# Seven products instead of eight blocks in the remaining chunks of a down-projection

## The chip, the cores and the metric

The kernel runs on one core of one Trainium2 chip. The metric is the device time of one execution in microseconds; lower is better. The core has a matrix engine (TensorE, "PE" in the profile, with its weight loads as "PEld"), a vector engine (VectorE, "DVE"), a scalar engine (ScalarE, "ACT"), GpSimd ("POOL") and a queue processor (SyncE, "SP"). SP, ACT and POOL issue the transfers (DMAs) that move data between the chip's memory (HBM) and the core's.

## The reference

Two layers of an encoder work on x of 256 positions by 2048 channels, all in float32. Layer 0 has pooling and attention, layer 1 a matrix memory (mLSTM) scanned in both directions. Each is followed by the same gated MLP, and this case is about its last product:

```python
def conv_ffn(x, w_up, conv_w, conv_b, w_down):
    u = x @ w_up                                   # 2048 -> 2 * 5632
    up = jnp.pad(u, ((0, 0), (1, 1), (0, 0)))
    u = c[0] * up[:, :-2] + c[1] * up[:, 1:-1] + c[2] * up[:, 2:] + conv_b
    gate, val = jnp.split(u, 2, axis=-1)
    return (jax.nn.silu(gate) * val) @ w_down      # 5632 -> 2048
...
x = x + conv_ffn(rms_norm(x, norm_ffn[layer]), w_up[layer], ...)
```

The down-projection multiplies a 256 x 5632 matrix by a 5632 x 2048 one.

## The kernel before

**Numbers.** Every float32 operand is held as a high and a low part (`hl[:, 0]` and `hl[:, 1]`), and a product of two operands is three matmuls: high by high, high by low, low by high. Weights arrive as chunks `w` of 128 x 1024 floats (512 KB). `Stream.split` (lines 119 to 131) makes the parts: ACT copies the rounded high part (line 127), DVE subtracts it for the low part (line 128). There are six `w` buffers and four `hl` buffers; the program loads five chunks ahead of the one in use and splits two ahead.

**Order of the work.** TensorE's instructions stand in the order in which the Python program emits them. The other engines' orders are chosen by a scheduler at build time. Each engine works in its order. Small work that must be spread in time is fed through `Weave`, a clock that the emission moves on: a product counts 0.68, one k tile of an up-projection 0.645 (microseconds, as the program supposes them), and a task runs when its time on that clock has come.

**The MLP.** `ffn_layer` runs six chunks of the inner dimension, of 4, 8, 8, 8, 8 and 8 tiles of 128 (`FCH`). For each tile, `up` makes gate and value (64 matmuls), the convolution and the gate on ACT and DVE, and a tile of `g`. The down-projection of chunk c is put between the up-projections of chunk c+1, in slots that `_ffn_plan` lists; chunk 5 has its own tail (`down_two`, `down`) after them. A chunk is taken apart into pairs of tiles: two in chunk 0, four in the others. The 2048 output columns form two halves, h = 0 and h = 1, of two blocks of 512.

- **Directly** (`down`, tile `dn`): per pair and half, two tiles by two column blocks by two halves of the rows by three matmuls, that is 24 matmuls of 512 columns, and two chunks of weights. A chunk ends with four additions of 512 columns into x (line 437).
- **In seven products** (`unit`, tile `pp`; a Strassen-Winograd scheme on the 2 x 2 blocks of a pair): four products in a unit of kind A, three in kind B, 21 matmuls. The left-hand combinations (`combine`, line 1004 on) serve both halves. B needs one and a half chunks of plain weights per pair. A needs two chunks of weight combinations per pair, and these are made in two ways:
  - for h = 1 by `Sum` and `Chain`: SP loads one weight chunk into a `sum` tile, POOL issues a second DMA that adds another to it (lines 112 and 113; three `sum` buffers, prepared up to ten chunks ahead), and DVE then adds the sum to a third chunk (lines 123 and 124);
  - for h = 0 by `premix` (line 464 on): long before use, five DMAs per pair make both combinations in HBM (`m`): two copies from ACT's queue (512 KB each), then from POOL's an accumulating one of 512 KB and two of 256 KB (line 473). SP loads the finished chunks later as any other (`w<-m`). Each of the five waits, by `paced`, for the matmul emitted last before it.

The products of a unit stay in PSUM over all pairs of a chunk; `drain` then adds them to `acc` or x in seven steps per chunk and half (line 1070; the first use of an `acc` tile is a copy on ACT, line 1068), and `total` ends a half after chunk 4.

**Which half goes which way.** `_halves` (line 1227) gives h = 1 the seven products in chunks 0 to 4 of both layers. h = 0 gets them in chunks 2, 3 and 4 of layer 0 and 1 to 4 of layer 1 (`BOTH`) and is done directly in the rest. When both halves go this way, a unit takes two pairs, and the eight slots of a chunk are A, A, B, B for h = 1 and the same for h = 0; otherwise a unit takes one pair, and `down` is appended to some slots.

**When the premixing is done.** `premix(layer, gap, late)` gives pair i the start `min(i + 1, 8) * gap + max(i - 7, 0) * late` on the clock; its five DMAs stand 0.2, 1.2, 1.2 and 1.2 gaps apart. In layer 0 (gap 26, late 90) it starts after the first projection of the attention, in layer 1 (28, 28) with the mLSTM.

Of the kernel before, what the change touches and what calls it, by code (L numbers as in the profile page):

```python
# [31 lines left out]
FT = DFF // P  # L32
FCH = [4, 8, 8, 8, 8, 8]
CH = 8
BOTH = ((2, 3, 4), (1, 2, 3, 4))
NEG = -1.0e30
NGATE = 96 + 8
WARM = 5
# [171 lines left out]
def trunk(ctx: ExitStack, tc: tile.TileContext, gx, xT, xn, call, catt, cml, weights, mixes, out):  # L210
# [249 lines left out]
    def paced(ins):  # L460

        tc.add_manual_dep(ins.ins, last_mm[0].ins.name, now, reason="paced")

    def premix(layer, gap, late):

        def one(i, s0, s1, r, made):
            m = scratch.tile([P, 2, CH * P], F32, tag=f"m{layer}{i}", name=f"m{layer}_{i}")
            h = CH * P // 2
            steps = [(nc.scalar, m[:, 0], s0, {}, 0.2), (nc.scalar, m[:, 1], r, {}, 1.2),
                     (g, m[:, 0], s1, add, 1.2), (g, m[:, 1, :h], m[:, 0, :h], add, 1.2),  # L470
                     (g, m[:, 1, h:], m[:, 1, :h], add, 0.0)]
            for eng, to, src, kw, wait in steps:
                paced(eng.dma_start(to, src, **kw))
                if wait:
                    yield wait * gap
            for j in range(2):
                made[j].ap = m[:, j]

        for i, e in enumerate(mixes[layer]):
            wv.aside(one(i, *e), min(i + 1, 8) * gap + max(i - 7, 0) * late)  # L480


    def attention_layer(norm, nxt):
        with ExitStack() as es:
# [239 lines left out]
            catb.extend(actp.tile([P, 8, 2, S], F32R, tag=f"B{i}", name=f"cat{i}") for i in range(2))  # L724
            wv.add(k_block(ps))
            wv.tick(0.0)
            premix(0, 26.0, 90.0)
            with tc.manual_schedule(engines={mybir.EngineType.SP}):
                ps = mov_group(xx, "qproj0", after=squares)
            wv.add(q_block(ps, 0, 5.5))  # L730
# [231 lines left out]
    def ffn_layer(layer, norm, nxt):  # L962
        with ExitStack() as es:
# [188 lines left out]
            for kind, c, i, *j in _ffn_plan(layer):  # L1152
                if kind == "up":
                    if i == 0:
                        gts.append(actp.tile([P, 8, 2, S], F32R, tag=f"B{c % 2}", name=f"g{layer}_{c}"))
                    up(c, f, gts[c], i)
                    f += 1
                elif kind == "down":
                    down(c, i)
                elif kind == "two":  # L1160
                    down_two(c)
                elif kind == "mix":
                    combine(c, i)
                else:
                    unit(kind, c, i, *j)

    norms = [Norm(0), None]
    norms[1] = Norm(1)
    attention_layer(norms[0], norms[1])
    norms.append(Norm(2))  # L1170
    ffn_layer(0, norms[1], norms[2])
# [54 lines left out]

def _halves(layer, c):

    return () if c in (-1, len(FCH) - 1) else (0, 1) if c in BOTH[layer] else (1,)


def _ffn_plan(layer):

    seq = []
    for c, n in enumerate(FCH):
        pairs = FCH[c - 1] // 2 if c else 0  # L1240
        halves = _halves(layer, c - 1)

        if halves == (0, 1):
            slots = [[(kind, c - 1, h, js)] for h in (1, 0) for kind in "AB" for js in ((0, 1), (2, 3))]
        else:
            slots = [[(kind, c - 1, 1, (j,))] for kind in "AB" for j in range(pairs)]
            for b in range(2 if pairs else 0):
                slots[(b + 1) * pairs // 2 - 1].append(("down", c - 1, b))

        busy = {j: k for k, slot in enumerate(slots) for u in slot if u[0] == "A" for j in u[3]}  # L1250
        for i in range(n):
            seq.append(("up", c, i))
            seq += slots[i] if i < len(slots) else []
            if c < len(FCH) - 1:
                seq += [("mix", c, j) for j in range(n // 2) if i == max(2 * j + 1, busy.get(j, 0))]
    return seq + [("two", len(FCH) - 1, 0)] + [("down", len(FCH) - 1, b) for b in range(2, NB)]


def _down_chunks(layer, w):


    out, k0 = [], 0
    for c, n in enumerate(FCH):
        rows = w[k0 * P : (k0 + n) * P]
        blocks = [_mov(rows[:, b * 512 : b * 512 + 512]) for b in range(NB) if b // 2 not in _halves(layer, c)]
        if c == len(FCH) - 1:
            b0, b1 = blocks[:2]
            blocks[:2] = [b0[:-1], b1[:-1], b0[-1:], b1[-1:]]
        out += blocks
        k0 += n  # L1270
    n = sum(FCH[:-1]) // 2
    res = [np.concatenate(out)]

    def two(a, b):
        return np.concatenate([a, b], axis=2)

    for h in range(2):
        b = w[: 2 * n * P, 1024 * h : 1024 * h + 1024].reshape(n, 2, P, 2, 512)
        b11, b12, b21, b22 = (b[:, k, :, c] for k in range(2) for c in range(2))
        res += [two(b12, b12), two(b11, b22), two(b22, b21), two(b11, b21), two(b22[::2], b22[1::2])]  # L1280
    return res


def _ffn_weights(layer, up, parts):

    down = iter(parts[0])
    out, u, mixes = [], 0, []
    for kind, c, i, *j in _ffn_plan(layer):
        if kind == "up":
            out += up[u : u + 4]  # L1290
            u += 4
        elif kind in ("down", "two"):
            out += [next(down) for _ in range(FCH[c] // 2 * (2 if kind == "two" else 1))]
        elif kind != "mix":
            q0 = sum(FCH[:c]) // 2
            s0, s1, r, ba, bb = parts[1 + 5 * i : 6 + 5 * i]
            js = [q0 + e for e in j[0]]
            if kind == "B":
                last = bb[js[0] // 2]
                out += [ba[q] for q in js] + [last if len(js) == 2 else last[:, js[0] % 2 * 512 : js[0] % 2 * 512 + 512]]  # L1300
                continue
            for q in js:
                if i:
                    out += [Sum(s0[q], s1[q]), Chain(r[q])]
                else:
                    made = [Made(), Made()]
                    mixes.append((s0[q], s1[q], r[q], made))
                    out += made
    return out, mixes
# [103 lines left out]
```

## Time and profile before

| | us |
|---|---|
| median of 3 runs | 2169.69 (2166.5 to 2171.02) |
| profiled execution, its own time | 2166.59 |
| span of its profile | 2164.4 |
| PE busy in the span | 2158.2 (100%) |
| DVE busy | 1726.4 (80%) |
| ACT busy | 1407.6 (65%) |
| POOL busy | 129.5 (6%) |

The span runs from the first to the last instruction of the core; the execution's own time has 2.2 us around it. In the profile, `up` is a tile of an up-projection, `dn` a direct down-projection, `pp` one of the seven products, `m` a premixed chunk in HBM, `sum` a sum made on the way in. All matmuls have line 264, since one helper emits them. The MLP of layer 0 lies at about 257 to 976 us, that of layer 1 at about 1450 us to the end.

### The profile page before, as it was taken

How to read it: one execution, taken by the hardware profiler on the slowest of the kernel's cores; microseconds unless marked ns; L12 is line 12 of the kernel's file. 1: busy time of each engine (PE TensorE's matmuls, PEld its weight loads, DVE VectorE, ACT ScalarE, POOL GpSimd, SP SyncE). 2: the span in 40 equal slices, each digit the busy share in tenths (PEclk: the TensorE clock that was granted, in tenths of full speed). 3: DMA queues.
4: the chain of work that ended last, by engine and by line, in shares of the span. 5: the costliest groups of instructions: out<-in, count | busy, mean ns of one | idle time of the engine just before them, and what ended most of it. 6: DMA issues, size and time to landing. Idle time of an engine off the chain costs nothing.

```text
span 2164.4 us, 31559 instructions
## 1 busy us (share of the span) xinstructions
PE 2158.2 (100%) x11424; PEld 1847.8 (85%) x11424; DVE 1726.4 (80%) x2415; ACT 1407.6 (65%) x2204; POOL 129.5 (6%) x160
## 2 busy tenths in 40 slices
PE   9999999999999999999999999999999999999999
PEld 8888888888888888889888888888888888888887
DVE  7686688887988888986777677667889898988896
ACT  7665576766777767666454544457677777776763
POOL 0011010000000000000000010110000000000000
PEclk9999999999999999999999999999999999999999
DMA  9678989787988877767688888998979787887774
GB/s 324 216 205 256 288 249 261 227 276 241 296 268 290 280 257 231 252 192 225 204 248 250 250 245 240 274 281 255 270 208 286 256 283 244 267 262 252 230 252 162
DMA packets 158079, 543.73 MB, mean 251 GB/s; under 512 B 17658, under 2 KB 20258, under 8 KB 157922
## 3 DMA queue, kind: packets, MB, share of 16 engines
q1 hardware_dynamic: 129056, 459.74, 62.2%
q0 software_dynamic: 17440, 48.51, 13.8%
q10 hardware_dynamic: 11426, 33.47, 4.8%
q8 instruction: 89, 1.46, 0.3%
q14 instruction: 68, 0.56, 0.1%
HBM read 539.50 MB, written 60.86 MB: 277 GB/s over the span
## 4 chain that ended last, share of the span: by engine, by line
PE 97%; DMA 1%; DVE 1%; issue 0%; ACT 0%; DVEq 0%; POOLq 0%; ACTq 0%
PE up L264 44%; PE pp L264 13%; PE op L264 8%; PE dn L264 6%; PE mv L264 4%; PE mq L264 4%; PE mk L264 4%; PE mo L264 4%; PE qproj L264 3%; PE kproj L264 1%; PE vproj L264 1%; PE pool L264 1%; DVE hl L128 1%; DMA sum<-in_dn 1%; DMA w<-in_up 1%; PE qk L264 1%
## 5 line engine op out<-in xcount | busy, mean ns | idle before, releaser
L128 DVE TENSOR_TENSOR hl<-w,hl 128x1024 fp32r<-128x1024 f32 (+2 forms) x836 | 1001.7, 1211 | 227.2 <-ACT hl L127 224.7
L127 ACT CAST hl<-w 128x1024 fp32r<-128x1024 f32 (+2 forms) x835 | 856.3, 1043 | 453.1 <-PE up L264 149.2
L264 PE MATMUL up<-xx,hl 128*128 128x512 f32 (+1 forms) x5632 | 994.1, 337 | 0.1
L264 PEld LDWEIGHTS up<-xx,hl 128*128 128x128 f32 x5632 | 867.0, 188 | 131.0 <-DVE hl L128 0.5
L264 PE MATMUL pp<-hl,s 128*128 128x512 f32 x768 | 192.7, 392 | 0.0
L264 PEld LDWEIGHTS pp<-hl,s 128*128 128x128 f32 x768 | 141.6, 188 | 29.0
L264 PE MATMUL pp<-hl,g 128*128 128x512 f32 x576 | 148.0, 391 | 0.0
L427 ACT COPY tb_up<-up 128x512 f32<-128x512 f32 x88 | 51.7, 587 | 124.5 <-PE up L264 124.3
L264 PEld LDWEIGHTS pp<-hl,g 128*128 128x128 f32 x576 | 105.4, 188 | 20.8
L264 PE MATMUL dn<-hl,g 128*128 128x512 f32 x528 | 122.7, 390 | 0.0
L264 PEld LDWEIGHTS dn<-hl,g 128*128 128x128 f32 x528 | 98.7, 188 | 20.4
L993 ACT ACTIVATE y<-tb_up,conv 128x256 f32<-128x256 f32 x176 | 103.9, 590 | 0.0
L994 DVE TENSOR_TENSOR y<-y,z 128x510 f32<-128x510 f32 x88 | 60.7, 689 | 54.2 <-ACT y L993 54.2
L428 DVE TENSOR_TENSOR tb_up<-up,tb_up 128x512 f32<-128x512 f32 x88 | 60.8, 690 | 50.5 <-ACT tb_up L427 49.9
L264 PE MATMUL mk<-xx,hl 128*128 128x512 f32 (+1 forms) x512 | 92.2, 337 | 0.0
L264 PE MATMUL mq<-xx,hl 128*128 128x512 f32 (+1 forms) x512 | 92.1, 337 | 0.0
L264 PE MATMUL mv<-hl,xx 128*128 128x512 f32 (+2 forms) x480 | 91.7, 350 | 0.0
L264 PE MATMUL op<-hl,cat 128*128 128x512 f32 x384 | 91.7, 393 | 0.0
L991 ACT ACTIVATE z<-tb_up,conv 128x256 f32<-128x256 f32 x176 | 88.6, 503 | 4.4 <-DVE tb_up L986 3.1
L264 PE MATMUL mo<-hl,xx 128*128 128x512 f32 x384 | 90.5, 391 | 0.0
L264 PE MATMUL op<-hl,mcat 128*128 128x512 f32 x384 | 89.5, 392 | 0.0
L264 PEld LDWEIGHTS mq<-xx,hl 128*128 128x128 f32 x512 | 79.2, 188 | 11.6
(232 smaller groups left out, 2092.7 us busy)
## 6 DMA issues: line engine op xcount, KB each, us to landing
w<-in_up SPq DMA_DIRECT2D x352, 512.0 KB, 4.7
w<-in_dn SPq DMA_DIRECT2D x176, 512.0 KB, 4.5
w<-in_m_in SPq DMA_DIRECT2D x124, 512.0 KB, 5.8
m<-in_dn ACTq DMA_DIRECT2D x56, 512.0 KB, 6.2
w<-m SPq DMA_DIRECT2D x56, 512.0 KB, 4.8
w<-in_a_in SPq DMA_DIRECT2D x46, 512.0 KB, 5.6
sum<-in_dn SPq DMA_DIRECT2D x36, 512.0 KB, 5.2
sum<-in_dn POOLq DMA_DIRECT2D x36, 512.0 KB, 8.9
```

Source lines behind the costliest of these rows:

```text
L127: (self.nc.vector.tensor_copy if i + c == 0 else self.nc.scalar.copy)(hl[:, 0, c : c + n], w[:, c : c + n])
L128: low = self.nc.vector.tensor_sub(hl[:, 1, c : c + n], w[:, c : c + n], hl[:, 0, c : c + n].bitcast(F32))
L264: last_mm[0] = pe.matmul(out_, lhsT, rhs, start=start, stop=stop, skip_group_check=True)
L427: a.copy(tb, ps[:, :, 1, :])
L428: v.tensor_add(tb, ps[:, :, 0, :], tb)
L991: a.activation(z[:, 0, j, :], u[:, j, :], AF.Copy, scale=cw(tl, 0))
L993: a.activation(y[:, j, :], u[:, j, :], AF.Identity, scale=cw(tl, 1), bias=cw(tl, 3))
L994: v.tensor_add(y[:, :, 1:S], y[:, :, 1:S], z[:, 0, :, 0 : S - 1])
```

## The change

Both halves now take the seven products in chunks 0 to 4 of both layers. New for h = 0 are chunks 0 and 1 of layer 0 (six pairs) and chunk 0 of layer 1 (two pairs). `_ffn_plan` is made to cope with a chunk of two pairs, whose slots are then one A and one B per half. Layer 0 premixes 18 pairs instead of 12, and those from the ninth on follow each other by 42 instead of 90 on the clock. Layer 1 premixes 18 instead of 16, with the same gap.

```diff
-BOTH = ((2, 3, 4), (1, 2, 3, 4))
...
-            premix(0, 26.0, 90.0)
+            premix(0, 26.0, 42.0)
...
 def _halves(layer, c):
 
-    return () if c in (-1, len(FCH) - 1) else (0, 1) if c in BOTH[layer] else (1,)
+    return () if c in (-1, len(FCH) - 1) else (0, 1)
...
         if halves == (0, 1):
-            slots = [[(kind, c - 1, h, js)] for h in (1, 0) for kind in "AB" for js in ((0, 1), (2, 3))]
+            slots = [[(kind, c - 1, h, js)] for h in (1, 0) for kind in "AB"
+                     for js in ((0, 1), (2, 3))[: pairs // 2]]
```

## The prediction

> **What bounds the kernel now.** I read the busy times first, then the chain of work that ended last, then what TensorE waited for, its matmuls in order of time, and last the transfers.
>
> ```profile
> span 2164.4 us, 31559 instructions
> PE 2158.2 (100%) x11424; PEld 1847.8 (85%) x11424; DVE 1726.4 (80%) x2415; ACT 1407.6 (65%) x2204; POOL 129.5 (6%) x160
> ...
> PE 97%; DMA 1%; DVE 1%; issue 0%; ACT 0%; DVEq 0%; POOLq 0%; ACTq 0%
> PE up L264 44%; PE pp L264 13%; PE op L264 8%; PE dn L264 6%; PE mv L264 4%; PE mq L264 4%; PE mk L264 4%; PE mo L264 4%; PE qproj L264 3%; PE kproj L264 1%; PE vproj L264 1%; PE pool L264 1%; DVE hl L128 1%; DMA sum<-in_dn 1%; DMA w<-in_up 1%; PE qk L264 1%
> ```
> ```profile
> PEld up L264 <- DVE hl L128: 0.5, 1, 0.5
> ```
>
> TensorE is the bound and has no gaps: of the waits of its weight loads only one, 0.5 us, lies in the MLPs. So a matmul taken out is a matmul's time gained, as long as weights still arrive. The single wait tells where that is closest to failing. The chain leads it back to a `sum`, its accumulating half, and a slow weight load:
>
> ```profile
> 679.00 5.16 DMA sum<-in_dn
> 684.73 8.83 DMA sum<-in_dn
> 706.53 13.73 DMA w<-in_up
> 722.71 8.18 PE up L264 x46
> ```
>
> **What is saved on TensorE.** These are stretches of one kind from the chain, start and length:
>
> ```profile
> 267.83 46.67 PE up L264 x268
> 317.28 5.44 PE dn L264 x24
> 355.26 11.14 PE up L264 x64
> 368.45 55.72 PE up L264 x320
> 440.85 10.88 PE dn L264 x48
> 554.34 5.53 PE pp L264 x24
> 587.67 4.10 PE pp L264 x18
> ```
>
> The direct half costs 5.44 us for 24 matmuls, 227 ns each. A unit of two pairs costs 5.53 us in kind A and 4.10 us in kind B. A unit of one pair is what lies between two rows: A from 314.50 (267.83 + 46.67) to 317.28, 2.78 us; B from 366.40 (355.26 + 11.14) to 368.45, 2.05 us.
>
> - A chunk of two pairs before: 2 x 2.78 + 2 x 2.05 + 2 x 5.44 = 20.54 us. After: 2 x (5.53 + 4.10) = 19.26. Saved: 1.28, in each layer, so 2.56.
> - Chunk 1 of layer 0 before: 4 x (2.78 + 2.05) + 2 x 10.88 = 41.08 us. After: 4 x (5.53 + 4.10) = 38.52. Saved: 2.56.
>
> Together 5.1 us, from 24 matmuls fewer. In a sentence of its own: the Trainium skill, page TensorE: Matmul & The Clock Gate, section Back-to-back issue gap, gives about 131 ns as the sustained spacing at 512 columns. By it the saving would be an estimated 3.1 us (24 x 0.131); the trace differs (227 ns), and the sum goes by the trace.
>
> **What is added beside TensorE.**
>
> ```profile
> L128 DVE TENSOR_TENSOR hl<-w,hl 128x1024 fp32r<-128x1024 f32 (+2 forms) x836 | 1001.7, 1211 | 227.2 <-ACT hl L127 224.7
> L127 ACT CAST hl<-w 128x1024 fp32r<-128x1024 f32 (+2 forms) x835 | 856.3, 1043 | 453.1 <-PE up L264 149.2 <-PE op L264 64.2 <-PE mo L264 38.4
> L1070 DVE TENSOR_TENSOR acc<-acc,pp 128x512 f32<-128x512 f32 x52 | 34.4, 680 | 0.0
> ```
> ```profile
> core 0: us, PE busy (x) PEld busy (x) DVE busy (x) ACT busy (x) POOL busy (x), PEclk, DMA share, GB/s
> 313.00:398.00 85.00, 85.00 (x462) 73.15 (x461) 69.33 (x95) 60.64 (x100) 6.73 (x8) 1.00 0.89 259
> 540.00:668.00 128.00, 128.00 (x685) 109.70 (x685) 112.66 (x148) 94.11 (x144) 6.70 (x8) 1.00 0.86 282
> 668.00:798.00 130.00, 129.94 (x691) 110.95 (x690) 115.78 (x153) 95.02 (x146) 6.77 (x8) 1.00 0.87 279
> 798.00:926.00 128.00, 128.00 (x683) 109.69 (x682) 115.13 (x144) 90.98 (x136) 0.87 (x1) 1.00 0.73 238
> ```
>
> - Splits: eight pairs need 3.5 weight chunks instead of 2, twelve splits more. DVE gets 12 x 1.21 = 14.5 us and ACT 12 x 1.04 = 12.5. DVE's additions from PSUM grow by some nine (seven drains per chunk and half instead of four, with the copies for a first use done by ACT in either kernel): 6 us. On average this lies beside TensorE: the three later rows are stretches with both halves in seven products, DVE is at 88 to 90%, and TensorE waits 0.06 us in 386. The same load is what chunks 0 and 1 get. Cost 0. If that cover went, the splits of A slots would be late first.
> - PSUM: the products use the four `ps` banks, and the drains finish during the next up-projection as they do now. Cost 0.
> - SP: twelve more loads' worth of weights. They pass through the same six buffers, at the mean rate of the three later rows. Cost 0 taken alone.
> - Premixing: eight pairs more, each two copies on ACT's queue and three accumulating DMAs on POOL's, and in layer 0 more than twice as dense from the ninth pair on. ACT and POOL wait for a matmul before each; the scheduler put them where ACT would wait anyway, and 56 such copies stand in ACT's order now with no wait of TensorE from it. Their issue costs 0. What the transfers do to others is the open cost.
>
> **The open cost: who meets the denser premixing.**
>
> ```profile
> w<-in_dn SPq DMA_DIRECT2D x176, 512.0 KB, 4.5
> m<-in_dn ACTq DMA_DIRECT2D x56, 512.0 KB, 6.2
> sum<-in_dn SPq DMA_DIRECT2D x36, 512.0 KB, 5.2
> sum<-in_dn POOLq DMA_DIRECT2D x36, 512.0 KB, 8.9
> m<-in_dn POOLq DMA_DIRECT2D x28, 512.0 KB, 8.4
> ...
> q1 hardware_dynamic: 129056, 459.74, 62.2%
> q0 software_dynamic: 17440, 48.51, 13.8%
> ```
>
> POOL's queue (q0) takes 13.8 / 48.51 = 0.284% per MB, the loads' (q1) 62.2 / 459.74 = 0.135: an accumulated byte costs the transfer engines 2.1 times a loaded one.
>
> Three sums of an h = 1 unit are prepared a whole chunk early; the fourth waits for the first buffer to come free, and that is tight. DVE and then POOL around it, in chunk 3's first two slots:
>
> ```profile
> 677.76 1.22 DVE L128 TENSOR_TENSOR hl<-sum,hl 128x1024 fp32r<-128x1024 f32 x1
> ...
> 693.58 0.69 DVE L123 TENSOR_TENSOR w<-w,sum 128x512 f32<-128x512 f32 x1 [2.17 <-DMA sum<-in_dn]
> ...
> 700.94 1.22 DVE L128 TENSOR_TENSOR hl<-w,hl 128x1024 fp32r<-128x1024 f32 x1
> ```
> ```profile
> 701.24 2.22 PE L264 MATMUL pp<-hl,s 128*128 128x512 f32 x9
> ```
> ```profile
> 418.20 0.81 POOL L473 DMA_DIRECT2D m<-in_dn  x1 [27.05 <-PE up L264]
> ...
> 513.66 0.81 POOL L473 DMA_DIRECT2D m<-in_dn  x1 [27.54 <-PE up L264]
> ...
> 675.29 0.81 POOL L473 DMA_DIRECT2D m<-m  x1 [32.45 <-PE up L264]
> 684.73 0.87 POOL L113 DMA_DIRECT2D sum<-in_dn  x1 [8.62 <-DMA sum<-in_dn]
> ```
>
> The buffer is free at 679.0, DVE wants the sum at 691.4 (693.58 - 2.17): 12.4 us. SP's half and POOL's half take 5.2 and 8.9 at the median, 14.1 with nothing between them. Here an `m` of 256 KB left POOL at 675.29 just ahead, and the sum came 2.17 us late. TensorE did not feel that at once: the split that follows from it ended at 702.16 (700.94 + 1.22), and the matmuls that use it begin 1.38 us (a quarter of the 5.53) after 701.24, at 702.62. So the lead is 2.17 + 0.46 = 2.6 us; what a sum is late beyond that, TensorE waits.
>
> Now where the premix falls. The two POOL rows at 418.20 and 513.66 are the ninth and tenth pair, 95.5 us apart for a step of 90, so the clock runs 1.06 slow and a step of 42 is 44.6 us. The ninth pair starts 48 earlier (250 instead of 298), so its POOL copy is at 367; the next ones at 412, 456, 501, 546, 590, 635, 679, 724, 768, each with two smaller ones 33 and 66 us later and two ACT copies 39 and 33 us earlier. The first A slots after the change are near 423, 551, 679 and 806 (a chunk's length is 8 x 11.14 + 38.5 = 127.6 us), and the fourth sum is in flight from some 3 us before to 11 us after:
>
> - chunk 1 (420 to 434): two ACT copies (418, 423), a small `m` at 434;
> - chunk 2 (548 to 562): a 512 KB `m` on POOL at 546, ACT copies at 551 and 557;
> - chunk 3 (676 to 690): a 512 KB `m` on POOL at 679, ACT copies at 685 and 691;
> - chunk 4 (803 to 817): a small `m` at 801.
>
> In layer 1 the two more pairs bring an `m` at about 1629, after the fourth sum of chunk 1 has gone, and chunk 0 needs only the sums prepared early: cost 0.
>
> A 512 KB transfer at the best rate seen over 16 us below (349 GB/s) is 1.5 us, an accumulating one 2.1 times that, 3.2 us.
>
> ```profile
> 570.00:586.00 16.00, 16.00 (x87) 13.65 (x85) 15.52 (x20) 10.94 (x17) 2.53 (x3) 1.00 1.04 345
> 586.00:602.00 16.00, 16.00 (x89) 13.78 (x88) 13.33 (x20) 12.64 (x20) 0.00 (x0) 1.00 0.95 349
> ```
>
> Bounds for each of chunks 1 to 3: nothing, if the sum still comes within its lead; at most the two copies and the accumulation whole, 2 x 1.5 + 3.2 = 6.2 us on top of no lead left. I take lateness 3 for chunk 1 and 4.5 for chunks 2 and 3, nearer to the row at 693.58 (2.17, after half as much traffic): stalls 0.4, 1.9 and 1.9, together 4.2. Chunk 4 is like the row: 0. The 0.5 us wait now at chunk 3 is contained in its new one, so 3.7 are new. Sum: -5.1 + 3.7 = **-1.4 us**. The profiled execution would go from 2166.59 to 2165.2; its time is 3.1 below the median of 2169.69, which goes to about **2168.3**.
>
> **The rivals.**
>
> - *The whole saving shows.* The sums stay within 2.6 us of lateness, as all did before. For it: in the stretch 570 to 602 the transfers ran at 345 and 349 GB/s with two premix pieces in it and nothing stalled. Against it: three of four meetings are denser than the one that was 2.17 late. Time: 2169.7 - 5.1 = 2164.6.
> - *Slower: the fourth sum falls behind the premix on POOL's queue.* A sum's second half is in the same queue as `m`; if it begins only when the `m` ahead has landed, and the ACT copies take a share too, it lands after as much as
>
> ```profile
> DMA to landing us min/median/max: 3.5/7.1/16.3
> ```
>
>   16.3 us, the longest of its kind. With 5.2 for the first half that is 21.5 against 12.4: 9.1 late, less the lead 6.5 us of stall, three times 19.5, net +14: 2184. It decides when the three stalls exceed 9.4 us together (5.1 saved and 4.3 of the bound below), 3.1 each, lateness 5.7. Against it: SP's loads run meanwhile and slow it only in part. Beside this stands, from the Trainium skill, DMA: Bandwidth & Descriptors, section Queues, rings and completion order, that each transfer engine takes its queues in turn, a packet at a time: a third active queue would then leave the sum a third where it had half. No row here shows three queues in turn packet by packet.
> - *The premix is not ready when its chunk is to be loaded.* SP would stand still with all weights behind it. The last pair's last `m` is at 768 + 66 = 834 and is needed from about 870 on; pairs of chunk 1 are as early as now. I give it 2 in 100.
>
> **How the numbers follow.** A change of under 0.2% (4.3 us) is about what a measurement of this kernel can't tell from none. My forecast, stalls between 0.8 and 9.4 us so that the net stays within that: 0.47. The whole saving, by over 0.2%: 0.31, as 5.1 is just above 4.3. Slower by over 0.2%, the POOL queue with the unready premix: 0.22. The range begins at the whole saving less half the runs' scatter (about 1): 2163.5, and reaches into the slower case to the point where each of the three sums is 7 us late (13.2 in stalls, net +8) less its far tail, leaving out 1 in 10: 2177. The likeliest case alone has 2165.4 to 2174.0.
>
> **What would show it.** 24 matmuls fewer in `dn` and `pp` together; 192 fewer `dn`, 168 more `pp`. Right: the fourth add of line 123 waits for `sum` near 435, 562 and 690, 2 to 5 us each, and TensorE's waits for line 128 grow from 0.5 to about 4 us, all in layer 0. If TensorE's waits stay under 1 us, the whole saving shows and I was wrong on the lateness. If the waits come behind `w<-m` on SP, the premix was late. If they come in layer 1, or in slots of h = 0, I have missed a cause.

## The result and the profile after

The changed kernel is slower: 2182.90 us at the median of four runs (2181.31 to 2183.69) against 2169.33 for the kernel before (2166.50 to 2171.02), a ratio of 1.0067 with a 95% interval of 1.0055 to 1.0079. I had forecast 2168.3 in a range up to 2177. The profiled execution took 2181.31 us; its span is 2179.5, 15.1 more than before. (Line numbers are one lower than before: the matmuls have line 263, the splits 126 and 127, the add of a sum 122.)

The page of the changed kernel, busy times and queues, then the waits of its weight loads (total us, times, longest):

```profile
span 2179.5 us, 31660 instructions
PE 2161.0 (99%) x11400; PEld 1845.0 (85%) x11400; DVE 1742.6 (80%) x2432; ACT 1418.6 (65%) x2212; POOL 149.5 (7%) x184
...
q0 software_dynamic: 20896, 56.90, 15.8%
```
```profile
PEld pp L263 <- ACT s L1013: 9.0, 2, 4.5
PEld pp L263 <- DVE hl L127: 5.2, 7, 1.7
PEld up L263 <- DVE hl L127: 2.6, 5, 0.8
PEld pp L263 <- DVE s L1014: 2.4, 2, 1.2
```

The 24 matmuls are gone (11424 to 11400). Where there was one wait of 0.5 us in the MLPs, there are now two kinds. The second and third line are the weight splits, which I had forecast. The first and last are new: `s`, a left-hand combination made by `combine`, twice each. TensorE in order of time (start, length, tile, count; in brackets idle time before and what ended it), at the first A unit of chunk 0 in layer 0:

```profile
314.23 2.24 PE L263 MATMUL pp<-hl,s 128*128 128x512 f32 x9
316.31 0.86 PE L263 MATMUL pp<-hl,g 128*128 128x512 f32 x3
321.20 1.22 PE L263 MATMUL pp<-hl,s 128*128 128x512 f32 x2 [4.04 <-ACT s L1013]
322.91 3.35 PE L263 MATMUL pp<-hl,s 128*128 128x512 f32 x7 [0.48 <-DVE s L1014]
326.06 1.28 PE L263 MATMUL pp<-hl,g 128*128 128x512 f32 x3
327.18 11.30 PE L263 MATMUL up<-xx,hl 128*128 128x512 f32 x64
```

The unit takes 12.95 us (314.23 to 327.18); the same unit for h = 0 starts at 353.55 and takes the 5.53 of the prediction. Of the 7.4 us too much, 4.5 are the two waits. The rest is in the matmuls behind them: seven in 3.35 us where nine took 2.24. The windows around it (us, busy time and count of each engine, granted clock, DMA share, GB/s) show why:

```profile
317.00:319.00 2.00, 0.17 (x1) 0.00 (x0) 2.00 (x4) 2.00 (x6) 0.00 (x0) 1.00 0.90 170
319.00:321.00 2.00, 0.00 (x0) 0.00 (x0) 1.81 (x4) 2.00 (x4) 0.86 (x1) 0.78 0.95 182
321.00:323.00 2.00, 1.31 (x3) 0.59 (x3) 2.00 (x5) 0.76 (x3) 0.00 (x0) 0.50 0.96 287
323.00:325.00 2.00, 2.00 (x5) 1.61 (x6) 0.82 (x3) 0.95 (x2) 0.00 (x0) 0.50 1.00 266
325.00:327.00 2.00, 2.00 (x6) 1.51 (x6) 0.90 (x1) 1.98 (x3) 0.00 (x0) 0.51 1.04 262
327.00:329.00 2.00, 2.00 (x12) 1.72 (x11) 0.86 (x2) 1.09 (x2) 0.00 (x0) 1.00 0.80 256
```

TensorE stands from 317.2 on (316.31 + 0.86). Within the window from 319 the granted clock falls: its mean of 0.78 puts the fall from 1.00 to 0.50 at about 320.1. It stays at 0.50 to 327, for almost 7 us. The Trainium skill, TensorE: Matmul & The Clock Gate, section What's actually happening, lists two states, 4/8 and 8/8, and says that the lower one comes after at least one idle window of about 3.4 us. The 0.50 here agrees; the fall came sooner, 2.9 us after TensorE stopped.

The chain of waits shows `s` being made (start, length, what), and DVE's order the last step ahead of the cast:

```profile
317.21 0.42 ACT z L990
...
319.31 0.42 ACT y L992
319.74 0.90 issue
320.64 0.52 ACT s L1013
...
322.91 4.43 PE pp L263 x10
```
```profile
318.27 1.22 DVE L127 TENSOR_TENSOR hl<-w,hl 128x1024 fp32r<-128x1024 f32 x1
319.40 0.28 DVE L1009 TENSOR_TENSOR sf<-sf,s 128x128 f32<-128x128 f32 x1
```

ACT works through six activations of the convolution (lines 990 to 992, twice) and a split before it comes to the cast of the combination at 320.64 (that split is the chain's "issue"). DVE has its own part in it: the last subtraction of the combination stands behind a weight split and ends at 319.68. The last up-projection of chunk 0 had ended near 303.1 (the unit's start at 314.23, less one up-projection of 11.14 that lies between). So its pair's first casts were done 18 us later (321.16), while TensorE had work for 13.9: that one up-projection and the first pair's 2.8. Layer 1 shows the same thing at its chunk 0: [4.04] and [0.48] before the same matmuls, 12.60 us from 1516.46.

The other part of the loss is what I had expected, in layer 0. DVE's adds of the fourth sum, then TensorE at the first of them:

```profile
573.43 0.69 DVE L122 TENSOR_TENSOR w<-w,sum 128x512 f32<-128x512 f32 x1 [3.83 <-DMA sum<-in_dn]
...
704.10 0.69 DVE L122 TENSOR_TENSOR w<-w,sum 128x512 f32<-128x512 f32 x1 [3.82 <-DMA sum<-in_dn]
```
```profile
574.34 0.39 PE L263 MATMUL pp<-hl,s 128*128 128x512 f32 x1
576.11 2.47 PE L263 MATMUL pp<-hl,s 128*128 128x512 f32 x8 [1.38 <-DVE hl L127]
...
582.57 0.63 PE L263 MATMUL up<-xx,hl 128*128 128x512 f32 x2
```

The unit at 574.34 takes 8.23 us (+2.7). The one at 705.82 takes 7.16 (+1.6), and three up-projections lose 0.5, 0.6 and 0.1: 5.6 together. Sum of the span: +7.4 and +7.1 in the two chunks 0, +5.6 for transfers in layer 0, +0.5 in one up-projection of layer 1, -5.1 for the matmuls, -0.4 for a stall that before had: +15.1, of 15.1 measured.

### The profile page after: what moved, and what is told of

The parts are those of the page before. It is cut to its first block, busy times and chain, and to the rows that moved or that the text cites. A ratio compares the mean times of both kernels' runs of the same rounds, so it can differ in the third digit from the quotient of the medians.

```text
span 2179.5 us, 31660 instructions
## 1 busy us (share of the span) xinstructions
PE 2161.0 (99%) x11400; PEld 1845.0 (85%) x11400; DVE 1742.6 (80%) x2432; ACT 1418.6 (65%) x2212; POOL 149.5 (7%) x184
## 4 chain that ended last, share of the span: by engine, by line
PE 94%; DVE 3%; DMA 2%; ACT 1%; issue 1%; DVEq 0%; ACTq 0%
PE up L263 42%; PE pp L263 14%; PE op L263 8%; PE mv L263 4%; PE mq L263 4%; PE mk L263 4%; PE mo L263 4%; PE dn L263 4%; PE qproj L263 3%; DVE hl L127 2%; PE kproj L263 1%; PE vproj L263 1%; DMA sum<-in_dn 1%; PE pool L263 1%; DMA w<-in_up 1%; PE qk L263 1%
## 5 line engine op out<-in xcount | busy, mean ns | idle before, releaser
L127 DVE TENSOR_TENSOR hl<-w,hl 128x1024 fp32r<-128x1024 f32 (+1 forms) x844 | 1016.6, 1217 | 224.4 <-ACT hl L126 217.8
L126 ACT CAST hl<-w 128x1024 fp32r<-128x1024 f32 (+1 forms) x843 | 866.9, 1047 | 456.8 <-PE up L263 158.4
L263 PE MATMUL pp<-hl,s 128*128 128x512 f32 x864 | 222.5, 399 | 11.5 <-ACT s L1013 8.1
L263 PEld LDWEIGHTS pp<-hl,s 128*128 128x128 f32 x864 | 161.1, 191 | 49.3 <-ACT s L1013 9.0
L263 PE MATMUL pp<-hl,g 128*128 128x512 f32 x648 | 166.3, 392 | 0.0
L263 PEld LDWEIGHTS pp<-hl,g 128*128 128x128 f32 x648 | 119.6, 189 | 24.0
L472 POOL DMA_DIRECT2D m<-m x72 | 61.2, 850 | 568.7 <-PE up L263 320.1
L263 PEld LDWEIGHTS mk<-xx,hl 128*128 128x128 f32 x512 | 79.1, 188 | 11.4
```

The costliest lines, as they stand in the source:

```text
L126: (self.nc.vector.tensor_copy if i + c == 0 else self.nc.scalar.copy)(hl[:, 0, c : c + n], w[:, c : c + n])
L127: low = self.nc.vector.tensor_sub(hl[:, 1, c : c + n], w[:, c : c + n], hl[:, 0, c : c + n].bitcast(F32))
L263: last_mm[0] = pe.matmul(out_, lhsT, rhs, start=start, stop=stop, skip_group_check=True)
```

## The experiments

Two theories at first. **D** (dependence): the larger part is the merged first A unit of chunk 0, whose second pair ends with the chunk's last tile; `_ffn_plan` puts only one up-projection between that tile's and the unit, and that is too short for its combinations. **S** (sums): the smaller part is the fourth sum of chunks 1 to 3 meeting the premix, so it hangs on the phase of the premix. Later runs tested the premix as a whole. Medians; each ratio is against the kernel before, measured beside it:

| run | us | ratio (95%) |
|---|---|---|
| after | 2182.90 | 1.0067 (1.0055 to 1.0079) |
| e1_single | 2167.53 | 0.9996 (0.9987 to 1.0005) |
| e4_fill | 2175.92 | 1.0037 (1.0023 to 1.0051) |
| e3_layer1 | 2174.93 | 1.0032 (1.0019 to 1.0044) |
| e11_two_early | 2171.05 | 1.0017 (1.0008 to 1.0026) |
| e2_clear | 2171.77 | 1.0013 (1.0004 to 1.0022) |
| e2_meet | 2166.09 | 0.9990 (0.9981 to 0.9999) |
| e5_plain | 2160.36 | 0.9961 (0.9948 to 0.9975) |
| e9_before_plain | 2165.88 | 0.9990 (0.9980 to 0.9999) |
| e7_fourteen | 2165.23 | 0.9986 (0.9977 to 0.9995) |
| e8_early | 2162.43 | 0.9972 (0.9959 to 0.9984) |
| e10_earlier | 2169.19 | 1.0003 (0.9995 to 1.0012) |

**e1_single: chunk 0's first A unit taken apart.** The change, with the two pairs of that one unit in two slots, an up-projection between them, as in the kernel before:

```diff
         if halves == (0, 1):
             slots = [...]
+            if pairs == 2:
+                slots[:1] = [[("A", c - 1, 1, (j,))] for j in range(2)]
```

> Theory D (the dependence): in chunk 0 the first A unit takes both pairs one slot after the last up-projection of that chunk, and the combinations of its second pair are not ready; with one pair per A unit there, the second pair comes one up-projection later. D expects the two stretches of 24 matmuls that took 12.95 and 12.60 us to become 5.5 us of matmuls again in two parts, so 14.5 us less: 2182.9 - 14.5 = 2168.4, and no wait of TensorE for line 1013. Rival Q (ACT's queue and the transfers are late there because of the added splits and the premix): the wait moves with them and most of the 14.5 us stays, above 2178.

It took 2167.53, 15.4 us less than the change. TensorE at the same place, without a wait:

```profile
314.17 2.24 PE L263 MATMUL pp<-hl,s 128*128 128x512 f32 x9
...
316.94 11.30 PE L263 MATMUL up<-xx,hl 128*128 128x512 f32 x64
328.08 2.24 PE L263 MATMUL pp<-hl,s 128*128 128x512 f32 x9
```

D holds: the same products are made, in another order. With an up-projection between the two pairs, the second one's combinations are there in time, in both layers.

**e4_fill: the wait filled with work that is thrown away.** The change, with 16 matmuls into a PSUM tile nobody reads, just ahead of the second pair's products:

```diff
+if n == 2 and len(js) == 2 and kind == "A" and h == 1 and m == 4:
+    fill = mmp.tile([P, 2, 512], F32, tag="mm", name=f"fill{layer}")
+    for r in range(16):
+        mm(fill[:, 0], todo[0][1][0], wh, r == 0, r == 15)
```

> The changed kernel with 16 more matmuls of 512 columns (3.6 us), whose result nobody reads, in the gap of 4.2 us before the second pair's products in chunk 0 of each layer. Theory C (a part of the loss is the clock, granted at 0.50 for some 6 us after TensorE has stood still for 4 us): the filled gap stays as long, the clock stays at 1.00, and the 12 matmuls behind it take 2.8 us instead of 5.5: 2 x 2.7 = 5.4 us less, 2177.5. Rival: the slow matmuls are slow for another reason (their weights or combinations trickle in): no less than 2182.

More work, and 7.0 us faster than the change: 2175.92.

```profile
317.24 3.82 PE L263 MATMUL fill<-hl,s 128*128 128x512 f32 x16
320.89 2.27 PE L263 MATMUL pp<-hl,s 128*128 128x512 f32 x9
...
323.68 11.30 PE L263 MATMUL up<-xx,hl 128*128 128x512 f32 x64
```

The granted clock is 1.00 in all windows from 315 to 325. The unit ends 9.22 us after its start at 314.46, where it took 12.95. So the fill gives back 3.7 us of this layer's 7.4. Some 2.8 of them are the clock: in the change the twelve matmuls behind the wait have 1.22 + 3.35 + 1.28 = 5.85 us, the first twelve 2.24 + 0.86 = 3.10. The other 0.9 is again order: in this build the casts of line 1013 stand ahead of a split and start 5.5 us after the unit's start (319.95), not 6.4 (320.64).

**e3_layer1: the kernel before with this one part.** Only layer 1's chunk 0 gets both halves; layer 0 and its premixing are as before:

```diff
-BOTH = ((2, 3, 4), (1, 2, 3, 4))
+BOTH = ((2, 3, 4), (0, 1, 2, 3, 4))
...
-            slots = [... for js in ((0, 1), (2, 3))]
+            slots = [... for js in ((0, 1), (2, 3))[: pairs // 2]]
```

> The kernel before with only chunk 0 of layer 1 changed (both pairs in the first A unit; layer 0 and its premix as before). Theory D with C (the second pair's combinations come 4 us late and the clock drops behind the wait): one stretch of 24 matmuls grows by 7.1 us, 1.3 are saved: 6 us over the kernel before. Rival T (the loss is mostly the traffic of layer 0): within 1 us of the kernel before.

2174.93, 6.4 us over the kernel before measured beside it, with the 1.3 us of matmuls saved in it.

```profile
1516.95 1.22 PE L264 MATMUL pp<-hl,s 128*128 128x512 f32 x2 [4.04 <-ACT s L1014]
1518.65 3.35 PE L264 MATMUL pp<-hl,s 128*128 128x512 f32 x7 [0.49 <-DVE s L1015]
```

The wait needs nothing of layer 0 and nothing of its denser premixing.

**e11_two_early: the merged unit kept, layer 0's premix moved.** The change with `premix(0, 22.0, 48.0)`:

```diff
-            premix(0, 26.0, 42.0)
+            premix(0, 22.0, 48.0)
```

> The changed kernel (both pairs in chunk 0's first A unit) with the premix at 22 and 48. If the two losses are independent, the shift gives what it gave behind single pairs, 5.1 us: 2177.8. If the wait of the first A unit hangs on the transfers, it shortens with them: below 2172.

2171.05: 11.9 us less than the change, where the moved premix alone gave 5.1 (e1 to e8, below). In layer 0 the merged unit lost only 1.3 us, in layer 1 as much as ever. In layer 0 here, the combination's last subtraction on DVE, its casts on ACT, and TensorE:

```profile
314.73 0.28 DVE L1009 TENSOR_TENSOR sf<-sf,s 128x128 f32<-128x128 f32 x1
```
```profile
315.23 0.51 ACT L1013 CAST s<-sf 128x384 fp32r<-128x384 f32 x1
...
316.60 0.30 ACT L1013 CAST s<-sf 128x128 fp32r<-128x128 f32 x1
...
317.74 0.51 ACT L990 ACTIVATE z<-tb_up,conv 128x256 f32<-128x256 f32 x1
```
```profile
313.30 2.24 PE L263 MATMUL pp<-hl,s 128*128 128x512 f32 x9
...
317.75 1.88 PE L263 MATMUL pp<-hl,s 128*128 128x512 f32 x7 [1.06 <-DVE s L1014]
```

The unit starts at 313.30. The subtraction comes 1.4 us later, in the change 5.2 (319.40 - 314.23), with DVE's weight splits ahead of it; the casts stand ahead of ACT's six activations, in the change behind them. The wait is 1.06 us, and the clock stays at 1.00. So D is sharper now: with this order of DVE and ACT the dependence leaves about 1 us of wait. The other 3.5 of the 4.5 go with their order in the change, which the scheduler fixes when the kernel is built and which here moved with an edit elsewhere. That order was not tried by itself.

**e2_clear and e2_meet: the phase of the late pairs.** e1 with the pairs from the ninth on 40.2 apart, placed to miss the fourth sums (from 250) or to meet them (11.8 later):

```diff
-    def premix(layer, gap, late):
+    def premix(layer, gap, late, phase=0.0):
...
-            wv.aside(one(i, *e), min(i + 1, 8) * gap + max(i - 7, 0) * late)
+            wv.aside(one(i, *e), min(i + 1, 8) * gap + max(i - 7, 0) * late + (i > 7) * phase)
...
-            premix(0, 26.0, 42.0)
+            premix(0, 26.0, 40.2, 1.8)     # e2_meet: 13.6
```

> As the kernel with one pair per A unit in chunk 0, and the premix of the late pairs of layer 0 every 40.2 on the clock from 250 on, a third of a chunk's 120.6, so that every chunk's fourth sum is in flight between an ACT copy and the next POOL transfer. Theory S (the sums meet the premix): DVE's waits for a sum, 3.83 and 3.82 us, go away and with them the 5.8 us that TensorE loses in chunks 1 to 3 of layer 0: about 2163 to 2164. Rival B (the transfers as a whole are too many at this density, whatever their place): the density is 4% higher, and the loss stays or grows: 2168 to 2170.

> The same with all these pairs 11.8 later, so that POOL's 512 KB transfer leaves just ahead of the fourth sum in every chunk and the two ACT copies follow during it. Theory S: DVE waits for the sum in all four chunks, about 4 us each, TensorE loses 1.5 to 2.5 us each: 6 to 10 us over the kernel with clear places. Rival B: the same time as that one within 1 us.

The other way round: 2171.77 for the one that should miss, 2166.09 for the one that should meet. The first did not clear the sums: DVE still waited 1.70 and 3.91 us for them, where e1 has 3.60 and 4.48. Beside that, ACT's splits waited for weights of the up-projection (25.7 us in 16 waits; 11.4 in 12 in e1), and a whole up-projection came apart, 15.6 us where 11.1 are usual. In the second, DVE's adds waited for the plain chunk, not for the sum. First the longer wait for a sum, the waits of ACT and one stretch of TensorE in e2_clear, then DVE in e2_meet:

```profile
699.62 0.69 DVE L122 TENSOR_TENSOR w<-w,sum 128x512 f32<-128x512 f32 x1 [3.91 <-DMA sum<-in_dn]
```
```profile
ACT hl L126 <- DMA w<-in_up: 25.7, 16, 4.3
```
```profile
723.89 2.94 PE L263 MATMUL up<-xx,hl 128*128 128x512 f32 x16
...
739.47 2.91 PE L263 MATMUL pp<-hl,g 128*128 128x512 f32 x12
```
```profile
567.09 0.69 DVE L122 TENSOR_TENSOR w<-w,sum 128x512 f32<-128x512 f32 x1 [3.50 <-DMA w<-in_dn]
```

S falls as it was stated: e2_meet has no wait for a sum, and yet its second A units of chunks 2 and 3 take 7.97 and 7.44 us for 5.53. At the same density, other loads were the late ones.

**e5_plain: the late premixing left out.** e1, with layer 0's ten pairs from the ninth on not premixed; SP loads plain chunks in their place, so every load, split and matmul remains:

```diff
+            if layer == 0 and i > 7:
+                e[3][0].ap, e[3][1].ap = e[0], e[2]
+                continue
```

> As the kernel with one pair per A unit in chunk 0, but the pairs of layer 0 from the ninth on are not premixed: SP loads the unmixed weights of the same size in their place, so that these products of h = 0 are not the reference's. All loads and splits stay; fifty premixing transfers of layer 0 go. Theory B (the transfers as a whole are too many at this density): the 6 to 7 us that TensorE loses in layer 0 shrink to under 1: 2162 to 2163. Rival L (the twelve added loads and splits are the cause): 2167 as with the premix.

2160.36, and the runs agree within 0.2 us (2160.22 to 2160.45). The MLP windows of layer 0 for the change, and for this run:

```profile
540.00:668.00 128.00, 125.83 (x662) 105.94 (x661) 111.23 (x147) 90.98 (x138) 10.83 (x13) 1.00 0.95 304
668.00:798.00 130.00, 129.14 (x685) 109.53 (x684) 114.13 (x151) 92.48 (x141) 10.10 (x12) 1.00 0.95 300
```
```profile
540.00:668.00 128.00, 128.00 (x684) 109.68 (x683) 114.92 (x152) 92.70 (x142) 3.40 (x4) 1.00 0.80 264
668.00:798.00 130.00, 130.00 (x696) 111.45 (x695) 116.96 (x154) 94.74 (x143) 3.41 (x4) 1.00 0.80 264
```

With 0.80 of the transfer engines in use instead of 0.95, TensorE loses nothing, and nearly all of the scatter from run to run goes too. Without the late premix the added splits, loads and drains are free. The late premix costs 2167.53 - 2160.36 = 7.2 us in e1.

**e9_before_plain: the same in the kernel before.** Its four late pairs not premixed, the rest as it was; the same three lines.

> The kernel before with the four late pairs of layer 0 not premixed (SP loads the unmixed weights of the same size, so that these products are not the reference's). Theory B says what the premix of layer 0 already costs there: the same kernel with all eight pairs more and no late premix took 2160.4, so this one should take 5.1 more, 2165.5, 3 below the kernel before, and its runs should lie within 0.5 us of each other as that one's did. Rival: the kernel before loses only the 0.5 us seen in its profile, and this takes 2168.

2165.88, against 2168.05 for the kernel before: it pays 2.2 us for its own late premix at the median, with an interval from 0.2 to 4.3. Nine of the ten runs lie within 0.8 us; the tenth, the profiled one, took 2167.59 and lost 1.6 us in one unit and the up-projection behind it, with no late premix at all. Between e9 and e5 lie the saved matmuls alone: 5.5 us.

**e7_fourteen: chunk 1 left direct.** e1 with h = 0 of layer 0's chunk 1 done directly, and `premix(0, 26.0, 72.0)`:

```diff
-    return () if c in (-1, len(FCH) - 1) else (0, 1)
+    return () if c in (-1, len(FCH) - 1) else (1,) if (layer, c) == (0, 1) else (0, 1)
```

> As the kernel with one pair per A unit in chunk 0, but chunk 1 of layer 0 does h = 0 directly as before: 14 pairs premixed in layer 0, the late ones every 72 on the clock. Theory B: 2.6 us of the 5.1 saved remain and the losses fall to about 1 us: 2 us below the kernel before, 2166. Rival L: the losses fall only by chunk 1's share and it stays at 2167 to 2168.

2165.23: giving up 2.6 us of saving gained 2.3 against e1, with four pairs fewer premixed and more room for the rest.

**e8_early and e10_earlier: more room by an earlier start.** e1 with the early pairs closer, during the attention, and the late ones farther apart:

```diff
-            premix(0, 26.0, 42.0)
+            premix(0, 22.0, 48.0)     # e10_earlier: 20.0, 50.0
```

> As the kernel with one pair per A unit in chunk 0, with the premix of layer 0 shifted to the attention: gap 22 instead of 26 and late 48 instead of 42, so 13% fewer transfers per time in the chunks. Theory B: some 2 to 3 of the 6.5 us lost come back: 2165. Rival (the place of single transfers decides): anywhere between 2164 and 2172, as a shift of 11.8 moved it by 5.7.

> One pair per A unit in chunk 0, and the premix of layer 0 shifted a step further: gap 20, late 50. Theory B: another 4% fewer transfers per time in the chunks than with 22 and 48, 0.5 to 1 us less: 2161.5 to 2162. Rival (the place of single transfers decides): up to 3 us either way.

e8 is the fastest version that computes the whole: 2162.43 (2161.15 to 2165.19), 6 us under the kernel before. A step of the same kind further, e10 gives it all back: 2169.19. It loses 2.9 us in an up-projection near 723, as e8 does near 715 (2.8). New is a loss in the attention, TensorE first, then a window with its clock:

```profile
160.38 0.58 PE L263 MATMUL ov<-pt,vt 128*128 128x256 f32 x1 [2.24 <-ACT pt L589]
161.83 1.44 PE L263 MATMUL ov<-pt,vt 128*128 128x256 f32 x5 [0.86 <-DVE pt L590]
163.06 4.73 PE L263 MATMUL op<-hl,cat 128*128 128x512 f32 x12
```
```profile
160.00:162.00 2.00, 0.76 (x2) 0.46 (x3) 2.00 (x4) 2.00 (x5) 0.00 (x0) 0.53 0.16 25
```

In the profiles, the first unit of the MLP starts 7.3 us later than in e8 (320.37, 313.08), and from there to the end of chunk 4 layer 0 takes as long in both (612.0, 611.7). So nearly all that e10 loses against e8 lies ahead of the MLP.

**What stays open.** That the late premix costs 2 to 11 us over e5 is shown; what decides the amount is not. It isn't the density of the late pairs alone (e2_clear and e2_meet have the same), nor the fourth sum alone (e2_meet). The share of the transfer engines doesn't decide it either: in the window from 540 to 668, e8 lost 0.3 us at 0.96, where the change lost 2.2 at 0.95. Twelve microseconds of shift changed the time by 5.7. A list of the places that matter would need a run for each.

## Why the prediction was wrong

- **The step that failed** is the one on the chunk of two pairs, "After: 2 x (5.53 + 4.10)", which put the first A unit of chunk 0 at the price of a unit whose inputs are ready. I had taken 5.53 from a chunk of four pairs; there the first unit takes pairs 0 and 1 of four, which are done long before. In chunk 0 the second of two pairs ends with the last tile of the chunk. `combine` was in none of my terms: its instructions are neither removed nor added, only wanted an up-projection sooner. This cost 7.4 + 7.1 us, and e1 takes it away. Without it, the forecast of 2168.3 stands beside 2167.53.
- **The size of it** came in part from the clock (2.8 of the 7.4 us in layer 0; in e4 it stayed at 1.00), which I had not counted for any wait. The Trainium skill, TensorE: Matmul & The Clock Gate, section Why this matters for your kernels, says to leave no idle gaps over about 3 us between bursts. The gap of 4.04 us agrees; in e10 2.24 us were enough, so here the bound is lower.
- **The rivals** did not hold it. Slower by POOL's queue was the wrong mechanism: the median landing of a sum's second half, on POOL's queue, went from 8.9 to 9.3 us only, that of its first half, on SP's, from 5.2 to 6.8. The unready premix did not occur. Only the last part of the prediction had it, as a sign of a missed cause: "If they come in layer 1".
- **The saving, 5.1 us,** was right: 24 matmuls fewer, 5.5 us between e9 and e5. So were the costs of nothing for splits, loads, PSUM and drains (e5).
- **The open cost** was near in size: waits of 3.8 us at chunks 2 and 3 as forecast (2 to 5), but none at chunk 1, and 5.6 us lost in place of 4.2. Against a median run, the added premix costs 5.0 (7.2 in e1 less 2.2 in the kernel before). As a mechanism it was wrong: I had counted three meetings of one kind of transfer, and in e2 other loads were late too, the plain chunk and the up-projection's weights. That the size came out near, and 2168.3 beside 2167.53 with it, is in part luck.
- **The profile of before** showed 0.5 us of stall, and I took it as the kernel's. That execution, 2166.59 us, is at the fast end of the runs; the median has some 2 us more, which e9 shows to be the premix.

## What to carry to other kernels

When work units are merged or moved forward, look up for each operand when it is made, on which engine and behind what, even if nothing is added to that engine; a duration taken from a unit with early inputs doesn't hold for the first one behind its producer. Count a standstill of TensorE of 4 us as the wait and more than half as much again for the slow clock behind it. Background transfers can cost time somewhere even if each has room by itself (here with the transfer engines busy to 0.95; in e5, without the late ones, at 0.80, nothing was lost), so test them by leaving them out, and don't take the stalls of one profile for the median's.

## What I had not expected of the hardware

The clock at 0.50 outlasted the standstill: it went on for about 6 us after a wait of 4.0 us. In e10 2.24 us of idling, up to 160.38, were enough: the window from 160 has 0.53, and twelve matmuls after it took 4.73 us. Worked out from the means of windows of 2 us, the clock was low about equally long in three cases: 320.1 to 327.0, 1521.6 to 1528.4 (means of 0.91 and 0.89 from 1520 and 1528) and in e10 160.1 to 167.0 (0.53 and 0.76 from 160 and 166), 6.8 to 6.9 us each. A wait of 1.06 us in e11 left it at 1.00. And more matmuls made the kernel faster: 16 useless ones, 3.8 us, in each layer, and the time fell by 7.0.
